# A two-layer hybrid decoder step: another order at three places between stages (modulation loads, first projection units, the pool of split weights)

## The chip, the cores and the metric

The kernel runs on one core of a Trainium2 chip, as one launch. The metric is device time in microseconds of that launch; lower is better. A core has five engines with queues of their own: TensorE (PE; the load of its stationary operand is listed apart as PEld), VectorE (DVE), ScalarE (ACT), GpSimd (POOL) and SyncE (SP), which here issues nearly all DMAs. Each engine runs its queue in order; semaphores order the queues against one another.

## The reference

Two layers are computed for 1024 prompt tokens and 32 sample tokens (8 sequences of 4), feature width 1024, in float32. Per layer, cut to what matters here:

```python
mod = (jax.nn.silu(c) @ lp["w_ada"] + lp["b_ada"])[:, None, :]
sh1, sc1, g1, sh2, sc2, g2 = jnp.split(mod, 6, axis=-1)
h = rmsnorm(x, lp["norm1_g"]) * (1.0 + sc1) + sh1
p = split_cols(h @ lp["w_in"])
...
x = x + g1 * (concat(o_a, o_b, o_c, o_d) @ lp["w_out"])
h2 = rmsnorm(x, lp["norm2_g"]) * (1.0 + sc2) + sh2
x = x + g2 * ((silu(causal_dwconv(h2 @ lp["ffn_w_gate"])) * (h2 @ lp["ffn_w_up"])) @ lp["ffn_w_down"])
```

The four head groups are an RG-LRU, differential attention, sparse attention (an indexer scores all keys, the 256 best are kept) and gated linear attention. The outputs are the last norm of x and the new caches and states.

## The kernel before

**Data.** x is kept transposed, xT[p, k, t], eight tiles of 128 features by 1056 tokens; the 1056 tokens go in three chunks, CHK = 384, 384 and 288 (the last holds 256 prompt tokens and the 32 sample tokens), or in nine tiles TOK of 128 (the last of 32). A float32 product is made of three: the weights and the activations are each split in a rounded part hi and a rest lo, and hi·hi, hi·lo and lo·hi are summed in PSUM.

**Weights.** `unit` (L426) loads a block of 1024 x 256 weights in two halves ("wr", two buffers, a DMA from SP each), ScalarE rounds each half to wh (L434), GpSimd subtracts to get wl (L435). wh and wl have two buffers each. `dense_t` (L456) and `dense_c` (L444, matmuls at L451) give output features by tokens, one chunk at a time, 24 matmuls; `dense_n` (L462, matmuls at L471) gives tokens by features, one token tile at a time, 24 matmuls.

**Head (L517 to L612).** The nine token tiles of x are loaded (512 KB each, "xn") and transposed to xT (L547); beside them go 20 small vector loads (`load_vectors`, L251) and the first four units of the modulation (`ada`, L317; 16 loads "adaw" of 512 KB in rows of 2 KB, 32 matmuls at L330, and a small transpose at L336, L338). Squares are summed per chunk (`add_square`, L346). Then `norm_chunk` (L385) runs for chunks 0, 1 and 2: the reciprocal root (`rstd_chunk`, L361), a VectorE product per feature tile (L392), and `split` (L375), which writes hi on ScalarE (L382, or L378 and L379) and lo on VectorE (L383) or GpSimd (L380), in turns. The six parts of h lie in a pool opened where the loads' pool was.

**Input projection (L633 to L1207).** Its pool "hp" is opened there, and holds wh and wl too. First comes `misc_unit` (L679): 128 odd columns (gla_a, idx_k, idx_w) for all three chunks, then nine transposes (L691), evacuations (L694, L695), rotations and stores, by token tile. Then `nat_unit("idx_q")` (L651): nine token tiles, each evacuated (L660), rotated (L499 to L503) and stored (L665). The tile "nat" that is stored has three buffers, shared by both units. The rotation table "c_rope" is loaded into hp. Then follow the units lru_x, lru_gate, dsa_q and so on. After each of their chunks or tiles, and after each idx_q tile, `background` (L639) advances other streams: the indexer, the top-k of the prompt and the samples, and in layer 0 one piece of the remaining modulation (16 matmuls, "late").

**Output projection and MLP (L1992 to L2198).** w_out is split into four units in two right-hand pools, wo and wo2; the MLP's pool "ffp" holds its own wh and wl. The last norm chunk of the MLP's input (L2115) is issued with the first gate unit (L2114). Eleven blocks q of 256 hidden features run gate, up and, one block late, down: 24 groups (8 feature tiles, 3 chunks) of 6 matmuls at L2082, each added to xT on VectorE (`add_residual`, L480). The last two blocks' down products are done together, 12 matmuls a group, chunk by chunk, with the squares (L354, L355) and the next layer's norm behind each chunk (L2193 to L2197):

```python
                if pend is not None and q < 10:
                    w = down_w(pend[0])
...
                    last = [(down_w(9), pend[1]), (down_w(10), mids)]
...
            for c in range(3):
                for m in range(8):
                    down_mc(m, c, last)
                    add_square(xT, m, c, acc, sqt)
                finish(c)
```

**What sets the order.** The program's order gives priorities, and the framework's planner, which runs a timeline simulation as it builds, makes each engine's fixed queue out of them. Pools lie on two stacks; a tile of a new pool waits for the tiles that lay at its place.

Of the kernel before, what the change touches and what calls it, by code (L numbers as in the profile page):

```python
# [71 lines left out]
def _const_tables():  # L72
    """Tables and 0/1 masks that depend on shapes alone, one float32 array of 128 rows."""
# [67 lines left out]
def trunk(ctx, tc, io, out, dbg=None, depth=DEPTH, stop=99):  # L141
# [19 lines left out]
    def banks(**bufs):  # L161
        """the eight banks of PSUM dealt out anew: single ones by name, pairs as s; d and e stay open while they can."""
# [10 lines left out]
    def advance(gens, n=1):  # L173
        """n steps of the first streams of the list that are not done; False when none is left."""
        for _ in range(n):
            while gens:
                try:
                    next(gens[0])
                    break
                except StopIteration:  # L180
                    gens.pop(0)
        return bool(gens)

    def pipeline(gens, depth):
        """the streams one after another, up to depth of them at once, a step of each per step, oldest first."""
# [20 lines left out]
    def evac(dst, src, ratio=(1, 1)):  # L206
        """PSUM to SBUF on ScalarE or VectorE in turns."""
# [41 lines left out]
    vecp = ctx.enter_context(tc.tile_pool(reuse_waits="tile", name="vec", bufs=1))  # L249

    def load_vectors(l, wp):  # L251
        v = {}
        if True:
# [39 lines left out]
            pa = bank("m")  # L293
# [5 lines left out]
            # half the convolution: silu(2 z) = z (1 + tanh(z))  # L299
            dve.tensor_scalar(V[:, 128:216], V[:, 128:216], 0.5, None, op0=mult)  # L300
            pc = bank("m")
# [15 lines left out]
    def ada(adap, l, u0, u1, nb=2, ne=1, nk=8):  # L317
        """units of 512 columns of the modulation, in pieces of nk * 128 rows and 1024 / nk columns."""
        w_ = 1024 // nk
        for u in range(u0, u1):  # L320
# [13 lines left out]
            pm = bank("m")  # L334
            for j in range(4):
                pe.matmul(pm[:, 9 * j:9 * j + 9], lhsT=ev[:, j * 128:j * 128 + 128], rhs=sum4,  # L336
                          start=True, stop=True)
            dve.tensor_tensor(mods[l][:, 4 * u:4 * u + 4, :], pm[:, :36].rearrange("p (j c) -> p j c", j=4),  # L338
                              vecs[l]["b_ada"][:, 4 * u:4 * u + 4, None].to_broadcast([128, 4, 9]), op=add)

# [5 lines left out]
    def add_square(x, k, c, acc, tmp):  # L346
        """acc += x^2 for the features of tile k, chunk c of the tokens."""
# [13 lines left out]
    def rstd_chunk(get, acc, c):  # L361
# [3 lines left out]
        # 1 / sqrt(v), v = sum / D + eps: ScalarE's value, then a Newton step  # L365
# [9 lines left out]
    def split(hi, lo, y, bias, k):  # L375
        """hi + lo = y + bias, lo on VectorE or GpSimd in turns."""
# [8 lines left out]
    def norm_chunk(get, x, acc, c, A, mod, base, hi, lo):  # L385
        """hi + lo = modulated norm of x, chunk c of the tokens."""
# [16 lines left out]
    def part(wp, c, z):  # L403
        """tile for part z of [features, tokens], chunk c of the tokens."""
# [7 lines left out]
    def raw_piece(rp, aps, width, i, n, nr):  # L412
        """rows of piece i of n of a [1024, width] block of weights; aps: list of (column, AP)."""
# [11 lines left out]

    def unit(wp, rp, aps, width, n=2, first=None):  # L426
        """hi and lo of a block of weights, [128, 8, width]."""
# [10 lines left out]
    def split2(parts_, c, g, raw):  # L438
        """the parts of two tiles of features, chunk c of the tokens."""
# [4 lines left out]
    def dense_c(w, j, h, c, order=range(8)):  # L444
        """out^T[m, t] = sum_k w[k, m] h[k, t] for 128 columns m and chunk c of the tokens."""
# [16 lines left out]
    def dense_n(w, i, h):  # L462
        """out[t, m] = sum_k h[k, t] w[k, m] for token tile i, 256 columns."""
# [12 lines left out]
    def add_residual(x, m, c, p, gate, mod):  # L476
        """x += gate * p for 128 features m and token chunk c."""
# [48 lines left out]
    with tc.tile_pool(reuse_waits="tile", name="xin", bufs=9) as xi:  # L526
# [13 lines left out]
        for i, (t0, n) in enumerate(TOK):  # L540
# [9 lines left out]
            if i % 2:  # L550
                next(ups[i // 2])
# [3 lines left out]
        while advance(vl):  # L555
            pass
# [1686 lines left out]
```

## Time and profile before

| | |
|---|---|
| time, median of 3 runs (lowest to highest) | 3930.11 us (3924.64 to 3934.86) |
| span of the profiled execution, first to last instruction | 3915.6 us |
| own time of the profiled execution | not listed apart from its span; the median is 14.5 us above the span |
| busy: PE, DVE, ACT, POOL | 3549.8, 2461.3, 1510.5, 1387.5 us |
| mean granted TensorE clock (1 is 2.4 GHz) | 0.952 |

The profile lists what each engine was busy with and what its idle time waited for. Busy shares are averages over stages with different limits, so the reading below goes stage by stage. Matmuls overlap, so the mean duration of one is longer than the step from one to the next.

### The profile page before, as it was taken

The numbers are of one execution on the slowest core, as the hardware profiler recorded it, in microseconds if no ns is written. First come the engines' busy times: TensorE is split into PE (matmuls) and PEld (weight loads), VectorE is DVE, ScalarE is ACT, GpSimd is POOL, SyncE is SP. The second block draws the span as 40 slices with busy tenths as digits, with TensorE's granted clock in tenths as the row PEclk, the third lists the DMA queues.
The fourth block names the chain that finished last, engine by engine and source line by source line (L and its number), as shares of the span: only waits on it lengthen the run. The fifth ranks groups of instructions, "written<-read, shape, count | busy, mean of one in ns | idle before, by whom it ended". The sixth has DMA issues, their size and how long they took to land.

```text
span 3915.6 us, 66494 instructions
## 1 busy us (share of the span) xinstructions
PE 3549.8 (91%) x26004; PEld 3202.2 (82%) x26004; DVE 2461.3 (63%) x5614; ACT 1510.5 (39%) x3058; POOL 1387.5 (35%) x1241
## 2 busy tenths in 40 slices
PE   5998867899898999999979988688997899999998
PEld 3887765577788999999979877556786899999997
DVE  6379989676445454445553999996753545555555
ACT  4345644376533211211243556535763322112122
POOL 2344226534233222222323642564333222323231
PEclk7999988999999999999989999899998999999999
DMA  6542334546431333321113222546546011111111
GB/s 223 158 129 87 112 116 144 181 131 187 165 103 44 98 103 94 96 76 44 55 65 89 87 87 79 155 150 195 150 155 207 28 44 44 49 39 54 44 44 56
DMA packets 351155, 407.77 MB, mean 104 GB/s; under 512 B 93455, under 2 KB 294909, under 8 KB 350682
## 3 DMA queue, kind: packets, MB, share of 16 engines
q1 hardware_dynamic: 311930, 265.09, 22.5%
q0 software_dynamic: 38912, 138.43, 11.1%
q8 instruction: 205, 3.36, 0.4%
q14 instruction: 108, 0.88, 0.1%
HBM read 354.32 MB, written 58.04 MB: 105 GB/s over the span
## 4 chain that ended last, share of the span: by engine, by line
PE 66%; DVE 19%; DMA 4%; ACT 4%; issue 4%; POOL 1%; SPq 1%; another core or an unknown queue 0%; DVEq 0%; ACTq 0%; POOLq 0%
PE d L451 32%; PE m L2082 13%; PE m L1601 3%; PE d L471 2%; DVE tkb L799 2%; PE d L1334 2%; DVE tku L799 2%; PE e L1340 2%; PE e L1363 2%; PE m L1596 1%; PE d L330 1%; PE g L1700 1%; PE m L719 1%; DVE nat L499 1%; DMA xn<-in_x_prompt_dram 1%
## 5 line engine op out<-in xcount | busy, mean ns | idle before, releaser
L451 PE MATMUL d<-h,wh 128*128 128x384 f32 (+1 forms) x5856 | 1413.2, 327 | 69.2 <-ACT wh L434 26.2
L451 PEld LDWEIGHTS d<-h,wh 128*128 128x128 f32 x5856 | 1038.8, 192 | 86.2 <-ACT wh L434 31.5
L451 PE MATMUL d<-h,wl 128*128 128x384 f32 (+1 forms) x2928 | 947.4, 327 | 3.6 <-POOL wl L435 3.6
L451 PEld LDWEIGHTS d<-h,wl 128*128 128x128 f32 x2928 | 559.5, 191 | 7.8 <-POOL wl L435 6.7
L435 POOL TENSOR_TENSOR wl<-wr,wh 128x1024 fp32r<-128x1024 f32 (+1 forms) x172 | 376.7, 2208 | 357.5 <-ACT wh L434 345.5
L471 PE MATMUL d<-wh,h 128*128 128x256 f32 (+1 forms) x2304 | 462.5, 297 | 34.0 <-ACT nat L664 18.1
L480 DVE SCALAR_TENSOR_TENSOR xT<-m,mod,xT 128x384 f32<-128x384 f32 (+1 forms) x480 | 273.1, 572 | 228.8 <-PE m L2082 228.3
L471 PEld LDWEIGHTS d<-wh,h 128*128 128x128 f32 (+1 forms) x2304 | 372.0, 192 | 54.6 <-ACT nat L664 22.7
L2082 PE MATMUL m<-mh,wdh 128*128 128x384 f32 (+1 forms) x1056 | 349.2, 331 | 0.4 <-DVE xT L480 0.4
L2163 POOL TENSOR_TENSOR ml<-z,mh 128x384 fp32r<-128x384 f32 x132 | 133.5, 1031 | 605.7 <-ACT mh L2162 605.7
L2082 PE MATMUL m<-ml,wdh 128*128 128x384 f32 (+1 forms) x1056 | 343.3, 325 | 0.0
L2082 PE MATMUL m<-mh,wdl 128*128 128x384 f32 (+1 forms) x1056 | 342.1, 325 | 0.0
L471 PE MATMUL d<-wl,h 128*128 128x256 f32 (+1 forms) x1152 | 339.8, 295 | 0.0
L434 ACT CAST wh<-wr 128x1024 fp32r<-128x1024 f32 (+1 forms) x172 | 157.9, 955 | 238.7 <-PE d L451 174.5
L2134 DVE COPY fs<-G 128x2 f32<-128x2 f32 x44 | 50.9, 1158 | 285.2 <-ACT G L2130 285.2
L471 PEld LDWEIGHTS d<-wl,h 128*128 128x128 f32 (+1 forms) x1152 | 221.7, 192 | 8.0 <-issue 5.7
L2130 ACT COPY G<-d 128x384 f32<-128x384 f32 x132 | 57.1, 443 | 418.1 <-PE d L451 387.5
L2082 PEld LDWEIGHTS m<-mh,wdh 128*128 128x128 f32 x1056 | 199.6, 189 | 9.3 <-issue 7.0
L2082 PEld LDWEIGHTS m<-ml,wdh 128*128 128x128 f32 x1056 | 199.2, 189 | 1.5 <-issue 1.2
L2082 PEld LDWEIGHTS m<-mh,wdl 128*128 128x128 f32 x1056 | 199.3, 189 | 0.0
L2072 POOL TENSOR_TENSOR wdl<-wr,wdh 128x1024 fp32r<-128x1024 f32 x44 | 105.0, 2418 | 263.8 <-ACT wdh L2071 263.8
L1334 PE MATMUL d<-c_ident,kv 128*128 128x128 f32 x1024 | 171.8, 291 | 10.6 <-ACT s_wT L210 4.0
(532 smaller groups left out, 6740.4 us busy)
## 6 DMA issues: line engine op xcount, KB each, us to landing
adaw<-in_w_ada_dram SPq DMA_DIRECT2D x96, 512.0 KB
wr<-in_w_in_dram SPq DMA_DIRECT2D x48, 512.0 KB
wr<-in_ffn_w_gate_dram SPq DMA_DIRECT2D x44, 512.0 KB
wr<-in_ffn_w_up_dram SPq DMA_DIRECT2D x44, 512.0 KB
wr<-in_ffn_w_down_dram SPq DMA_DIRECT2D x44, 512.0 KB
xd<-xT SPq DMA_DIRECT2D x16, 528.0 KB
wr<-in_w_out_dram SPq DMA_DIRECT2D x32, 256.0 KB
mix<-mx SPq DMA_DIRECT2D x24, 256.0 KB
```

The source lines that it names most:

```text
L434: act.copy(hi[:, ks, :width], raw[:, :, :width])
L435: pool.tensor_tensor(lo[:, ks, :width], raw[:, :, :width], hi[:, ks, :width].bitcast(F32), op=sub)
L451: pe.matmul(pd, lhsT=w[a][:, k, j * 128:j * 128 + 128], rhs=h[b][c][:, k, :], start=(q == 0), stop=(q == 23))
L471: pe.matmul(pd[:n, :256], lhsT=h[b][c][:, k, t0:t0 + n], rhs=w[a][:, k, :], start=(q == 0), stop=(q == 23))
L480: dve.scalar_tensor_tensor(x[:, m, t0:t0 + n], p[:, :n], mod[:, gate + m, 0:1], x[:, m, t0:t0 + n], op0=mult, op1=add)
L799: dve.tensor_scalar(scratch[:, :n], src[:, s], thr[:, j:j + 1], None, op0=OP.is_ge, op1=add, accum_out=cnt[:, j:j + 1])
L1334: pe.transpose(pm[:, z_ * 128:z_ * 128 + 128], kg[:, j, f * 128:f * 128 + 128], ident)
L1340: pe.matmul(pd[32 * j:32 * j + 32, c], lhsT=Q[:, f, b_].rearrange("p c t -> p (c t)"), rhs=kt[:, j, f, :], start=(f == 0), stop=(f == 1))
L1601: pe.matmul(po[:, 64 * z:64 * z + 64], lhsT=wT[:, x * 128:x * 128 + 128], rhs=vn[:, kb, :], start=(kb == 0), stop=(kb == i))
L2072: pool.tensor_tensor(lo[:, z_, :], raw, hi[:, z_, :].bitcast(F32), op=sub)
L2082: pe.matmul(pd, lhsT=a, rhs=b, start=(n == 0), stop=(n == len(ops) - 1))
L2163: pool.tensor_tensor(ml[:, cs], z[:, cs], mh[:, cs].bitcast(F32), op=sub)
```

## The change

It does six things, all in the order of work and the place of tiles; every matmul stays.

- The first modulation is loaded by `ada_first`: eight loads of 1 MB, in rows of 8 KB, and its 32 matmuls run by row block over four PSUM banks. The loads, and the small vector loads, are issued after the third of the nine x tiles, ahead of the other six.
- `misc_unit` and the idx_q unit become `first_units`: chunk by chunk, the odd columns, three idx_q tiles, then the three transposes with their rotations and stores. It calls no `background`.
- wh and wl move from hp and ffp to a pool of their own, opened beside wr (`weights`), which spans output projection, MLP and the next input projection. The first two w_out units use it; wo2 is gone.
- The unit of odd columns is split before its stage (`mw`), not only loaded.
- In layer 0 the down product of block 9 is done like the others, and only that of block 10 runs chunk by chunk with the norm.
- The vectors' transposes take a "d" bank in the head.

```diff
@@ ada / ada_first
-            pm = bank("m")
...
+            ada_rows(l, u, ev)
+    def ada_first(adap):
+        pa = [bank("m") for _ in range(4)]
+        for k in range(8):
+            w = adap.tile([128, 2048], F32, name="adaw", bufs=8)
+            sp.dma_start(w, io["w_ada"][0][k * 128:(k + 1) * 128, 0:2048])
+            q = k % 4
+            for u in range(4):
+                pe.matmul(pa[u][32 * q:32 * q + 32, :], lhsT=cT[:, k, :], rhs=w[:, 512 * u:512 * u + 512],
+                          start=(k < 4), stop=(k >= 4))
+            yield
+        for u in range(4):
+            ev = adap.tile([128, 512], F32, name="adae", bufs=4)
+            evac(ev, pa[u])
+            ada_rows(0, u, ev)
@@ head
-        ups = [ada(xi, 0, u, u + 1, 16, 4, 2) for u in range(4)]
+        ups = [ada_first(xi)]
...
-            advance(vl, 3)
-            if i % 2:
-                next(ups[i // 2])
...
+            if i == 2:
+                advance(ups, 4)
+                advance(vl, 20)
+                advance(ups, 4)
+                while advance(vl):
+                    pass
+                while advance(ups):
+                    pass
...
-    mraw = raws(wrp, misc_aps(0), 128)
+    wrpool, wrp, wpool, wp_ = weights("0")
+    mw = unit(wp_, wrp, misc_aps(0), 128)
@@ input projection
-            w = unit(hp, wrp, [(0, col(name))], 256)
+            w = unit(wp_, wrp, [(0, col(name))], 256)
...
+        def first_units():
             rope_t.append(const("rope", where=hp).rearrange("p (i w) -> p i w", i=9))
+            w = unit(wp_, wrp, [(0, col("idx_q"))], 256)
             mtp = tc.tile_pool(reuse_waits="tile", name="mt", bufs=1)
             mt = mtp.__enter__().tile([128, T], F32, name="mt")
+            for c, (c0, cn) in enumerate(CHK):
+                act.copy(mt[:, c0:c0 + cn], dense_c(mw, 0, h, c))
+                for i in range(3 * c, 3 * c + 3):
+                    nat_tile("idx_q", w, i)
+                for i in range(3 * c, 3 * c + 3):
+                    t0, n = TOK[i]
+                    pm = bank("m")
+                    pe.transpose(pm[:n, :128], mt[:, t0:t0 + n], ident)
...
             sp.dma_start(stt["gla_a"], mt[0:16, :])
...
-        misc_unit()
-        nat_unit("idx_q")
+        first_units()
@@ output projection and MLP
-        wrpool = tc.tile_pool(reuse_waits="tile", name=f"wr{l + 1}", bufs=2)
-        wrp = wrpool.__enter__()
+        wrpool, wrp, wpool, wp_ = weights(f"{l + 1}")
...
-                    ws_.append(unit((wo, wo2)[u // 2], wo, [(0, io["w_out"][l][:, u * 256:u * 256 + 256])], 256, 4))
+                    ws_.append(unit((wp_, wo)[u // 2], wo, [(0, io["w_out"][l][:, u * 256:u * 256 + 256])], 256, 4))
...
-            w0 = unit(fp_, wrp, [(0, io["ffn_w_gate"][l][:, 0:256])], 256, first=graw)
+            w0 = unit(wp_, wrp, [(0, io["ffn_w_gate"][l][:, 0:256])], 256, first=graw)
...
-                if pend is not None and q < 10:
+                if pend is not None and (q < 10 or l + 1 < depth):
...
-                    last = [(down_w(9), pend[1]), (down_w(10), mids)]
+                    last = ([] if l + 1 < depth else [(down_w(9), pend[1])]) + [(down_w(10), mids)]
...
-                mraw = raws(wrp, misc_aps(l + 1), 128)
+                mw = unit(wp_, wrp, misc_aps(l + 1), 128)
```

## Rows read from the trace of the kernel before

**Rows 1.** The page: shares of the chain that ended last, by engine.

```profile
PE 66%; DVE 19%; DMA 4%; ACT 4%; issue 4%; POOL 1%; SPq 1%; another core or an unknown queue 0%; DVEq 0%; ACTq 0%; POOLq 0%
```

**Rows 2.** Windows: stretch, length, busy of PE, PEld, DVE, ACT, POOL; clock, DMA.

```profile
20.00:40.00 20.00, 14.67 (x87) 7.18 (x87) 11.35 (x24) 9.34 (x19) 1.05 (x2) 1.00 1.01 368
...
48.00:100.00 52.00, 23.73 (x64) 14.84 (x63) 42.42 (x78) 27.34 (x64) 23.96 (x30) 0.62 0.52 161
...
150.00:260.00 110.00, 110.00 (x997) 100.68 (x996) 62.61 (x82) 53.49 (x97) 35.13 (x35) 1.00 0.56 164
260.00:560.00 300.00, 256.78 (x1760) 231.17 (x1758) 288.17 (x780) 156.83 (x317) 115.24 (x114) 0.94 0.28 87
...
1994.00:2025.00 31.00, 27.73 (x179) 26.90 (x177) 27.47 (x61) 17.75 (x35) 6.66 (x6) 1.00 0.19 75
2025.00:2045.00 20.00, 1.52 (x3) 0.73 (x4) 14.30 (x35) 9.81 (x22) 5.69 (x7) 0.54 0.26 103
2045.00:2066.00 21.00, 20.78 (x125) 20.09 (x125) 3.16 (x5) 6.30 (x15) 12.80 (x12) 0.87 0.52 146
2066.00:2074.00 8.00, 1.67 (x5) 0.61 (x5) 2.19 (x13) 1.88 (x12) 2.72 (x14) 0.82 0.47 119
```

**Rows 3.** Timeline of the head: start, length, what, idle before and its releaser.

```profile
45.78 0.68 PE L547 MATMUL d<-c_ident,xn 32*128 32x32 f32 x8
...
47.84 0.19 DVE L338 TENSOR_TENSOR mod<-m,V 128x36 f32<-128x36 f32 x1
...
56.28 0.61 ACT L382 ACTIVATE h<-ny,mod 128x384 fp32r<-128x384 f32 x1
...
98.57 0.40 ACT L400 CAST h<-ny 128x256 fp32r<-128x256 f32 x1 [0.23 <-DVE ny L399]
```

**Rows 4.** Chain: first lru_x chunk, layer 0; idx_q tiles, lru_x, layer 1.

```profile
149.77 4.17 PE d L451 x24
...
2087.89 8.72 PE d L471 x72
2096.61 4.16 PE d L451 x24
```

**Rows 5.** Groups by shape: 1990 to 2045, 2044 to 2100, 100 to 150.

```profile
L480 DVE SCALAR_TENSOR_TENSOR xT<-m,mod,xT 128x384 f32<-128x384 f32 x8 | 4.9, 614 | 1.1 <-PE m L2082 1.0
...
L499 DVE TENSOR_TENSOR nat<-rraw,c_rope 128x256 f32<-128x256 f32 x8 | 4.8, 601 | 7.1 <-ACT rraw L660 6.3 <-DMA st_iw<-nat 0.7
...
L330 PE MATMUL d<-adaw,cT 128*32 128x128 f32 x144 | 5.8, 278 | 1.3 <-DVE nat L499 1.0 <-DMA adaw<-in_w_ada_dram 0.3
```

**Rows 6.** Line L872, last step of the top-k, both layers.

```profile
L872 DVE TENSOR_SCALAR mk<-tkb x5: 317/2446/2540, 527.1 to 556.4; 128x384 bf16<-128x384 bf16 x1, 128x512 bf16<-128x512 bf16 x1, 128x640 bf16<-128x640 bf16 x1, 128x768 bf16<-128x768 bf16 x1
...
L872 DVE TENSOR_SCALAR mk<-tkb x3: 363/386/415, 2484.8 to 2500.0; 128x768 bf16<-128x768 bf16 x1, 128x896 bf16<-128x896 bf16 x1, 128x1024 bf16<-128x1024 bf16 x1
```

**Rows 7.** Timeline of the boundary between the layers.

```profile
1970.94 0.42 PE L2082 MATMUL m<-mh,wdh 128*128 128x384 f32 x1
...
2024.24 0.30 PE L2082 MATMUL m<-mh,wdl 128*128 128x288 f32 x1
...
2043.80 0.40 ACT L400 CAST h<-ny 128x256 fp32r<-128x256 f32 x1 [0.25 <-DVE ny L399]
...
2045.07 0.33 SPq L220 DMA_DIRECT2D c_rope<-in_const_dram  x1
```

**Rows 8.** Waits on PE, 1970 to 2100: total, times, longest.

```profile
PE m L691 <- ACT nat L695: 5.8, 4, 4.4
```

**Rows 9.** Timeline of the start of the MLP, layer 0, then layer 1.

```profile
1195.07 2.53 POOL L435 TENSOR_TENSOR wl<-wr,wh 128x1024 fp32r<-128x1024 f32 x1 [2.69 <-DVE ny L370]
...
1195.41 2.52 DVE L372 TENSOR_TENSOR rb<-rb,ny 128x288 f32<-128x288 f32 x1
...
1210.74 1.25 PE L451 MATMUL d<-h,wh 128*128 128x288 f32 x3 [8.01 <-ACT h L400]
...
3124.72 1.25 PE L451 MATMUL d<-h,wh 128*128 128x288 f32 x3 [7.42 <-ACT h L400]
```

More of the change, by code (lines that the diff above doesn't have):

```diff
@@ L333, in ada, with ada_rows @@
                 yield
-            pm = bank("m")
[L335 to L339, printed above, removed]
+            ada_rows(l, u, ev)
+    def ada_rows(l, u, ev):
+        pm = bank("m")
+        for j in range(4):
+            pe.matmul(pm[:, 9 * j:9 * j + 9], lhsT=ev[:, j * 128:j * 128 + 128], rhs=sum4,
+                      start=True, stop=True)
+        dve.tensor_tensor(mods[l][:, 4 * u:4 * u + 4, :], pm[:, :36].rearrange("p (j c) -> p j c", j=4),
+                          vecs[l]["b_ada"][:, 4 * u:4 * u + 4, None].to_broadcast([128, 4, 9]), op=add)
+    def ada_first(adap):
[12 more added lines that the diff above has]
+            ada_rows(0, u, ev)
     def scales(g, mod, base, A):
@@ L424, in raws, with weights @@
         return [raw_piece(rp, aps, width, i, 2, 2) for i in range(2)]
+    def weights(name):
+        rp = tc.tile_pool(reuse_waits="tile", name="wr" + name, bufs=2)
+        wp = tc.tile_pool(reuse_waits="tile", name="w" + name, bufs=2)
+        return rp, rp.__enter__(), wp, wp.__enter__()
     def unit(wp, rp, aps, width, n=2, first=None):
@@ L554, in trunk @@
                     add_square(xT, k, i // 3, acc, sqt)
-        while advance(vl):
-            pass
-        for g in ups:
-            next(g, None)
+            if i == 2:
[6 more added lines that the diff above has]
+                    pass
     identb = cp.tile([128, 128], BF, name="identb")
@@ new lines, in first_units @@
+            for c, (c0, cn) in enumerate(CHK):
[3 more added lines that the diff above has]
+                for i in range(3 * c, 3 * c + 3):
+                    t0, n = TOK[i]
+                    pm = bank("m")
+                    pe.transpose(pm[:n, :128], mt[:, t0:t0 + n], ident)
+                    nat = hp.tile([128, CWM], F32, name="nat", bufs=3)[:, :256]
+                    raw = hp.tile([128, 256], F32, name="rraw", bufs=2)
+                    act.copy(raw[:n, 0:32], pm[:n, 32:64])
+                    act.copy(nat[:n, 32:40], pm[:n, 64:72])
+                    tmp = hp.tile([128, 256], F32, name="rtm", bufs=2)
+                    rope(nat[:n, 0:32], raw[:n, 0:32], i, n, 32, tmp[:n, 0:32], rope_t[0])
+                    sp.dma_start(st["idx_k"][t0:t0 + n, :], nat[:n, 0:32])
+                    sp.dma_start(st["idx_w"][t0:t0 + n, :], nat[:n, 32:40])
@@ L2003, in trunk @@
         ff = hpl.__enter__()
-        wrpool = tc.tile_pool(reuse_waits="tile", name=f"wr{l + 1}", bufs=2)
-        wrp = wrpool.__enter__()
+        wrpool, wrp, wpool, wp_ = weights(f"{l + 1}")
         with ExitStack() as es:
-            nm_, wo2, wo = (es.enter_context(tc.tile_pool(reuse_waits="tile", name=k, bufs=2, side="right"))
-                            for k in ("nm", "wo2", "wo"))
+            nm_, wo = (es.enter_context(tc.tile_pool(reuse_waits="tile", name=k, bufs=2, side="right"))
+                       for k in ("nm", "wo"))
             def staged(c, n):
```

69 lines of the change are left out of this document (28 added, 41 removed).

## The prediction

> **What bounds it now.** I read the chain first, then windows by stage, then timelines where TensorE stops. The chain is TensorE's for 66% [rows 1], and where it is busy throughout, at full clock, this change takes no matmul away; so I look for places where it waits. In the windows [rows 2] there are two large ones. In the head, 48 to 100 us, PE is busy 23.73 of 52 us at a clock of 0.62 while VectorE is busy 42.42: the three norm chunks feed it too slowly. Between the layers, 2025 to 2045, PE works 1.52 of 20 us at 0.54 while VectorE finishes the last norm; from 2066 to 2074 it works 1.67 of 8. Two small ones lie at the start of each MLP, 8.01 and 7.42 us [rows 9]. Saved time must then pass the stage behind. From 150 us PE is busy 110.00 of 110 us and then VectorE 288.17 of 300 [rows 2]; both depend on the first projection units alone, so the whole of it moves earlier. I count from the first lru_x chunk: 149.77 in layer 0, 2096.61 in layer 1 [rows 4].
>
> **The head, start.** Moving the modulation ahead of six x tiles leaves the bytes as they are, some 12.7 MB (8.4 of weights, 4.3 of x). The DMA ran at 368 GB/s and a share of 1.01 there with rows of 2 KB [rows 2], so I give rows of 8 KB no gain. The Trainium skill ("DMA: Bandwidth & Descriptors", Bandwidth) says to batch transfers to 1 MiB for three quarters of peak and lists 425 GB/s for the largest; by that the 12.7 MB would take 4.6 us less and the sum would be 3866. The 512 KB transfers here already ran at 368.
> What changes is what is last. Now the modulation is ready at 47.84, after the last x tile's transpose at 45.78, and the first part of h is written at 56.28 [rows 3]: in between lie the scale, the root, and a queue of squares. Afterwards modulation, root and squares of chunk 0 are done while x still lands. But chunk 0's hi part lies where I reckon the last x tiles lie, in the order in which the tiles are taken, so it cannot be written before about 46.5. That is 10 us earlier; the ends are 0 and, if it lies elsewhere, some 14.
> VectorE then has the same three norms plus the rotations of six idx_q tiles, which now come before the end of the last norm: 12 operations at 0.6 us [rows 5], 7 us. So the last part of h comes 3 us earlier than 98.57 [rows 3], near 96. SP carries the 20 vector loads ahead of x4 to x9; each is small and runs beside the 1 MB loads, so nothing is charged.
>
> **The head, behind the norm.** Now 50.8 us pass from the last part of h to lru_x (149.77 less 98.97). Afterwards one odd chunk and three idx_q tiles are left: 24 matmuls at 4.17/24 us times 288/384, 3.1 us, and 72 in 8.72 us [rows 4], 11.8 together at full clock and 23.7 at half. The clock has been 0.62 in this stage [rows 2] and more work fills it, so I take the middle, 18: 33 us less. The rest of the first units must fit under the norms: two odd chunks and six tiles, 26 us at full clock, in the 50 from 46 to 96; they fit at half clock too, barely.
> Nine pieces of later modulation leave this stretch (144 matmuls, 5.8 us busy [rows 5]) and follow later. From lru_x to the last step of the top-k, layer 0 takes 556.4 less 149.8, 406.6 us, with 23 such pieces; layer 1 takes 2500.0 less 2096.6, 403.4, with none [rows 4, 6]. So 23 cost at most 3.2 us and nine 1 us; the cover is the VectorE stretch, and without it they would cost 6.
> Head: -3 - 33 + 1 = -35 us; ends -49 and -17 (no earlier start, 7 for the rotations, half clock, 3 for the pieces).
>
> **Between the layers.** TensorE's sum is unchanged; block 9's pass just comes first. It takes 96 matmuls of 384 columns and 48 of 288, 23 us at the same step, so the chunk-wise pass begins not at 1970.94 [rows 7] but near 1994. VectorE's work behind it is 27.47 + 14.30 us [rows 2] and 9.6 for the 16 operations of chunk 0 that it now does before 1994 (at 0.6, L480's 614 ns [rows 5]): 51.4. Done densely it ends at 2045.4; with the 5.7 us of idle that 2025 to 2045 shows, at 2051, 7 later than 2044.2 [rows 7]. The extra 24 additions of block 9 hide under its matmuls.
> What TensorE does meanwhile is the gain. Odd chunks 0 and 1 fit before. The idx_q weights, though, need the wh buffer that block 10 gives up with its last matmul, near 2036 at VectorE's pace, and the rotation table seems to lie over the norm's scratch: its load is issued at 2045.07 [rows 7], right behind the norm, and will be again, some 4 us to landing (0.65 MB at 368 GB/s is 1.8; I take double for issue and completion). Four tiles can run without it, two in the evacuation buffers and two in PSUM. Left after the table: 3.1 + 5 x 2.9 = 18 us. lru_x then starts at 2051 + 4 + 18 = 2073 instead of 2097: -24.
> Against it: the splits of odd columns and idx_q, which now run where VectorE idles (3.16 of 21 us busy [rows 2]), move under its chain. A GpSimd split of 2.53 us stretched a VectorE operation to 2.52 [rows 9], where its like takes some 0.5. Two whole and two half splits: at most 7.6 us, and I take all of it, the chain being dense. Boundary: -16 us; ends -24 and +11 (the chain 23 later, nothing run ahead, locks on top).
>
> **The start of the MLP.** The first gate block's buffer is now free when the first w_out unit ends, several feature tiles before the end of that pass, so its split and the first up split can go earlier. They now sit in the last norm chunk: 2.52 us for L372 is one such collision [rows 9], 2 us too long, and I take the other half of that split to cost as much. Taking both away brings the norm's end 4 us forward in each layer: -8; ends 0 and -15 (both waits gone, 8.01 + 7.42). If the norm is not faster, TensorE only waits longer there, since it starts gate earlier.
>
> **Sum.** -35 - 16 - 8 = -59. The profiled span of 3915.6 becomes 3857; with the 14.5 us between span and median, 3930.1 becomes 3871.
>
> **Rivals.**
> *The boundary gives nothing* (0.20). VectorE's chain moves by the whole 23 us and nothing of idx_q runs ahead. For it: VectorE, 27.47 of 31 us, sets the pace there [rows 2]; against: some of its idle is waiting for TensorE. +3 to +11 for -16: about 3894. The Trainium skill ("SBUF — State Buffer", Who interferes with whom) says that a VectorE operation with two SBUF inputs and a GpSimd one that reads SBUF take a pair of ports by turns, whole instructions long; [rows 9] bear that out, 2.53 beside 2.52.
> *The head keeps its norm* (0.12). The part of h still waits for x, the clock stays half: -17 for -35, 3889. That rows of 8 KB do nothing belongs here, and is my assumption already. With the rival above, 3912.
> *The store buffers take turns with TensorE* (0.07; the other side). idx_q tiles and odd tiles now alternate over the three nat buffers, 18 a layer, six turns, and the transposes stand between the tiles in TensorE's queue. Now the wait shows for the odd tiles alone, 4.4 us at the longest [rows 8], and 6.3 us of idle from 2066 to 2074 [rows 2]. If every turn cost that, 12 x 6.3 = 76 us would come on: 3947, slower. It decides from 5.9 us a turn ((59 + 12)/12). Against it: 6.3 us of matmuls lie between two turns.
> The rest (0.06) is the planner dealing another stage out differently; the two layers' 406.6 and 403.4 us say that it deals alike.
>
> **Numbers.** The forecast has 0.55, and by itself 3850 to 3892. From the ends, -88 (3842) and -6; the range goes from 3842 to 3918, over the first two rivals, and leaves the third out. 0.3%, 12 us, is about what a measurement here can tell from no change. Faster by more: the forecast and most of two rivals, 0.84; within it 0.08, both rivals together or a mild third; slower 0.08.
>
> **What would show it.** Right: modulation ready before the last x transpose and the first h near 46; the first lru_x chunk near 114; between the layers the last norm 7 us later and lru_x 16 us earlier behind the start of block 9's pass than now; idx_q matmuls before the last norm ends; no split inside the MLP's last norm chunk. Wrong: first h still past 55; PE waits on nat at every transpose; the last norm between the layers more than 15 us later with TensorE idle beside it; VectorE no longer dense behind lru_x, so that what was gained is lost there.

## The result, and the profile after

| | before | after |
|---|---|---|
| median (lowest to highest), us | 3932.49 (3924.64 to 3936.61) | 3954.66 (3950.60 to 3964.66) |
| profiled execution: own time / span, us | - / 3915.6 | 3950.6 / 3948.8 |
| mean granted TensorE clock | 0.952 | 0.946 |

The ratio is 1.0062, interval 1.0043 to 1.0081: the change makes the kernel slower, where I forecast 3871 us and a range of 3842 to 3918. The two profiled spans differ by 33.2 us, the medians by 22.2: a part of the differences below belongs to the two executions that were profiled. (After's own time lies 1.8 us above its span, and in the later comparisons the kernel before has medians of 3916.6 to 3918.8. So the 14.5 us that I put between its span and its median were no fixed part of the time: executions of the same kernel differ by that much.)

To find where the time went I cut the span at four points in each layer, each read from one tile of the trace: the first store of lru_x, the last write to the top-k's tile tkb, the last load of w_out, the last mh (the rounded hidden features) of the MLP. "Mixers" are the four head groups. The columns after "after" are experiments that come below.

| us from the point before | before | after | head | units | pool | after_kb9 | after_kb9_vec | units_rows_kb9 |
|---|---|---|---|---|---|---|---|---|
| start to lru_x, layer 0 | 156.9 | 133.5 | 160.8 | 124.2 | 153.6 | 134.5 | 122.6 | 123.3 |
| to the end of the top-k | 407.8 | 431.5 | 408.1 | 429.2 | 405.7 | 431.7 | 431.5 | 432.5 |
| to w_out (the mixers) | 558.6 | 546.5 | 567.4 | 549.0 | 558.7 | 545.0 | 553.8 | 543.8 |
| to the last mh (output, MLP) | 849.7 | 854.9 | 853.4 | 853.5 | 854.8 | 852.9 | 856.3 | 854.1 |
| to lru_x, layer 1 (boundary) | 131.2 | 134.8 | 131.5 | 126.8 | 137.7 | 135.0 | 134.9 | 125.5 |
| to the end of the top-k | 395.0 | 400.1 | 394.9 | 395.4 | 394.8 | 395.1 | 400.0 | 396.8 |
| to w_out (the mixers) | 536.8 | 566.6 | 544.0 | 553.3 | 535.8 | 543.5 | 540.2 | 543.2 |
| to the last mh | 802.9 | 806.0 | 805.9 | 805.1 | 805.6 | 806.1 | 807.9 | 804.8 |
| to the end | 76.7 | 74.9 | 75.3 | 77.8 | 75.1 | 75.1 | 75.0 | 75.1 |
| span | 3915.6 | 3948.8 | 3941.3 | 3914.3 | 3921.8 | 3918.9 | 3922.2 | 3899.1 |

After less before: -23.4, +23.7, -12.1, +5.2, +3.6, +5.1, +29.8, +3.1, -1.8; sum +33.2. lru_x does start 23 us earlier, and all of it is gone by the end of layer 0's top-k. The boundary gives nothing. The largest term, +29.8, lies in the mixers of layer 1, where the source was not touched. Each column is one execution, so a few us prove little: before, pool and before_kb9 run the same order up to lru_x, and it comes at 156.9, 153.6 and 153.9.

**Head.** SyncE's queue, timeline of after (start, length, what):

```profile
3.67 2.17 SPq L350 DMA_DIRECT2D adaw<-in_w_ada_dram  x4
...
8.73 0.27 SPq L291 DMA_DIRECT2D va_rows<-in_lru_conv_w_dram  x1
11.21 0.23 SPq L291 DMA_DIRECT2D va_rows<-in_lru_conv_b_dram  x1
...
18.75 0.23 SPq L291 DMA_DIRECT2D va_rows<-in_lru_lambda_dram  x1
...
23.26 2.10 SPq L350 DMA_DIRECT2D adaw<-in_w_ada_dram  x4
...
25.88 5.07 SPq L568 DMA_DIRECT2D xn<-in_x_prompt_dram  x5
```

What SP waited for in it (total, times, longest):

```profile
SPq L291 <- DMA adaw<-in_w_ada_dram: 9.0, 4, 2.3
```

The same stretch, 0 to 48 us, in the DMA view (40 slices of 1.2 us, busy tenths and GB/s), and the first and the last step of the head's norm on ScalarE:

```profile
DMA  0247999999999980001489999999999999921404
GB/s 0 57 66 263 379 416 451 430 423 410 437 423 416 437 315 5 8 5 38 125 142 389 410 430 423 437 423 430 438 370 404 406 413 406 304 20 32 82 6 52
```

```profile
L402 ACT ACTIVATE h<-ny,mod x12: 492/602/615, 62.6 to 104.5; 128x384 fp32r<-128x384 f32 x8, 128x256 fp32r<-128x256 f32 x4
...
L420 ACT CAST h<-ny x1: 404/404/404, 109.3 to 109.3; 128x256 fp32r<-128x256 f32 x1
```

Behind four loads of 1 MB a small load comes off SP only every 2.5 us, because SP waits for landings. By the trace's semaphores the program lets each DMA of SP wait until the one eight places before it has landed, and the issues at 11.21, 13.69, 16.19 and 18.75 follow the landings of the four 1 MB loads by 0.02 us. Twelve more small loads then take until 23.26, when the fifth 1 MB load is issued. From 18.0 to 22.8 us, slices 16 to 19, the DMA engines move 5 to 38 GB/s, in the next two 125 and 142. The first part of h is written at 62.6, where it was at 56.28, and the norm ends at 109.3, where it ended at 98.57 [rows 3].

**Stages.** Windows of after (columns as in [rows 2]):

```profile
20.00:40.00 20.00, 15.70 (x42) 4.14 (x41) 1.36 (x3) 0.58 (x1) 0.00 (x0) 0.83 0.83 325
48.00:100.00 52.00, 36.36 (x174) 29.35 (x173) 44.28 (x74) 31.03 (x65) 20.96 (x21) 0.68 0.52 166
...
2040.00:2056.00 16.00, 0.00 (x0) 0.00 (x0) 10.91 (x22) 7.32 (x17) 5.59 (x7) 0.50 0.12 42
```

TensorE does work beside the head's norm now, 36.36 of 52 us for 23.73 [rows 2]. VectorE, which worked 11.35 us from 20 to 40, now works 1.36. And between the layers TensorE stands still for 16 us on end.

From lru_x to the top-k's first step, in before and then in after, same columns:

```profile
156.90:275.40 118.50, 117.43 (x1077) 107.49 (x1076) 70.90 (x94) 57.33 (x100) 37.11 (x39) 1.00 0.56 164
```

```profile
133.50:271.10 137.60, 130.72 (x1185) 116.78 (x1184) 71.33 (x101) 61.93 (x113) 42.52 (x46) 0.98 0.55 159
```

The first of six query blocks' scores on VectorE, in before and then in after (shortest, median, longest; first and last start):

```profile
L761 DVE TENSOR_SCALAR sc<-irl,wix x6: 402/620/917, 156.0 to 255.5; 128x384 f32<-128x384 f32 x1, 128x512 f32<-128x512 f32 x1, 128x640 f32<-128x640 f32 x1, 128x768 f32<-128x768 f32 x1
```

```profile
L793 DVE TENSOR_SCALAR sc<-irl,wix x6: 487/587/782, 153.7 to 250.2; 128x384 f32<-128x384 f32 x1, 128x512 f32<-128x512 f32 x1, 128x640 f32<-128x640 f32 x1, 128x768 f32<-128x768 f32 x1
```

VectorE has the same 71 us of work there, but the stretch is 19.1 us longer: TensorE works 13.3 us more in it, on 108 more matmuls that stand ahead of the top-k's start. (50 of them are of the later modulation, 38 of the projections, 20 of the scores themselves.) The first score comes only 2.3 us earlier than in before, 20.2 us behind lru_x, where it was level with it. The top-k itself then takes 4.6 us more.

**Boundary.** Timeline of after, GpSimd, VectorE, ScalarE and TensorE in turn:

```profile
2027.33 5.00 POOL L461 TENSOR_TENSOR wl<-wr,wh 128x1024 fp32r<-128x1024 f32 x2 [0.83 <-ACT wh L460]
...
2055.11 0.72 POOL L421 TENSOR_TENSOR h<-ny,h 128x256 fp32r<-128x256 f32 x1
...
2027.82 4.92 DVE L412 SCALAR_TENSOR_TENSOR ny<-xT,A,rb 128x384 f32<-128x384 f32 x2
...
2055.87 0.38 ACT L691 ACTIVATE rraw<-d 128x256 f32<-128x256 f32 x1 [0.86 <-POOL h L421]
2056.15 0.47 ACT L716 COPY mt<-d 128x384 f32<-128x384 f32 x1
...
2056.30 0.58 PE L497 MATMUL d<-wh,h 128*128 128x256 f32 x1 [17.72 <-ACT rraw L691]
```

One odd chunk and one idx_q tile were computed ahead (24 matmuls each, the last near 2034). They fill the two PSUM banks "d", and neither bank is emptied (rraw, mt) before the norm's very last operation, L421 at 2055.11, has read the norm's scratch. TensorE waits 17.72 us.

**Layer 1's mixers.** Last gathers of the samples and last transposes of the prompt, in before and then in after, there with the w_out loads, and the chain right behind:

```profile
L245 POOL DMA_INDIRECT kv<-in_cache_dsa_v_dram,idx x32: 935/939/1388, 2743.5 to 2974.2; - x32
...
L1263 PE MATMUL m<-c_ident,oa_dsa x16: 272/273/282, 2962.7 to 2973.8; 128*128 128x128 f32 x16
```

```profile
L245 POOL DMA_INDIRECT kv<-in_cache_dsa_v_dram,idx x32: 933/937/2825, 2769.0 to 3010.6; - x32
...
L1295 PE MATMUL m<-c_ident,oa_dsa x16: 272/273/328, 2972.7 to 2983.4; 128*128 128x128 f32 x16
...
L439 SPq DMA_DIRECT2D wr<-in_w_out_dram x16: 367/378/462, 3017.0 to 3067.9; - x16
```

```profile
3026.90 3.24 DMA mix<-s_oT
```

The prompt is done at 2983.4; the samples' last gather is issued 27.2 us later, and the chain runs through their store (mix<-s_oT). I call these 27.2 us the samples' tail. In before both ended together: 2974.2 for the gather, 2973.8 for the prompt. (The first expectations give 24 and 51 us for it; they count from an earlier step of the prompt, its last masked scores at 2950.3 and 2959.8.) Over all seventeen kernels of this document, the three with a tail of 27 us or more in layer 1 take 562.0 to 573.7 us in its mixers, and the others, with 7.4 at most, 535.8 to 553.6.

### The profile page after: what moved, and what is told of

The parts are those of the page before. It is cut to its first block, busy times and chain, and to the rows that moved or that the text cites. A ratio compares the mean times of both kernels' runs of the same rounds, so it can differ in the third digit from the quotient of the medians.

```text
span 3948.8 us, 66548 instructions
## 1 busy us (share of the span) xinstructions
PE 3566.9 (90%) x26004; PEld 3214.4 (81%) x26004; DVE 2478.8 (63%) x5654; ACT 1514.1 (38%) x3058; POOL 1395.5 (35%) x1241
## 5 line engine op out<-in xcount | busy, mean ns | idle before, releaser
L506 DVE SCALAR_TENSOR_TENSOR xT<-m,mod,xT 128x384 f32<-128x384 f32 (+1 forms) x504 | 286.7, 572 | 225.5 <-PE m L2113 225.0
L2194 POOL TENSOR_TENSOR ml<-z,mh 128x384 fp32r<-128x384 f32 x132 | 133.3, 1028 | 605.5 <-ACT mh L2193 605.5
```

The source lines that it names most:

```text
L506: dve.scalar_tensor_tensor(x[:, m, t0:t0 + n], p[:, :n], mod[:, gate + m, 0:1], x[:, m, t0:t0 + n], op0=mult, op1=add)
L2194: pool.tensor_tensor(ml[:, cs], z[:, cs], mh[:, cs].bitcast(F32), op=sub)
```

## The experiments

Ratios are against the kernel before, run beside each on the same chip.

**The parts alone.** Each is the kernel before with one part of the change's diff.

*head*: `ada_first` and its place in the loop over x.

```diff
-        ups = [ada(xi, 0, u, u + 1, 16, 4, 2) for u in range(4)]
+        ups = [ada_first(xi)]
```

> The kernel before with the head's part alone (modulation in 1 MB loads ahead of x3 to x8; units and pools as before). Theory A, 'the index keys set layer 0': the index scores start after the last chunk of the odd columns; here these stay ahead of idx_q, so idx_k is read back as many us earlier than 120.3 as lru_x is earlier than 156.9, and the top-k ends that much earlier than 564.7: if the last norm comes 3 to 6 us earlier, the total falls by 3 to 6 us. Theory B, 'the head itself is worse': TensorE's queue holds the modulation's matmuls ahead of the transposes of x3 to x8, the last norm comes no earlier than 98.6, and the total is 0 to +10 us. Theory C, 'the samples are dealt differently': the gap between the last prompt step and the last kv gather of layer 1 (24 us in before, 51 in after) moves by over 10 us though nothing in layer 1 was edited.

Ratio 1.0096 (1.0071 to 1.0120). The norm ends at 102.5, lru_x comes 3.9 us later, and everything up to the top-k's end is shifted by 4.2: theory B for the head, but not for the total, which rose by 32 us. The rest of the +25.7 us in span is in the mixers (+8.8 and +7.2) and the output and MLP stages (+3.7, +3.0), with nothing edited there. The samples' last gather, 0.4 us behind the prompt in both layers of before, is now 19.4 and 7.4 behind: a part of theory C.

*units*: `first_units` in place of the odd columns' unit and the idx_q unit, with its weights in hp.

```diff
-        misc_unit()
-        nat_unit("idx_q")
+        first_units()
```

> The kernel before with the first two projection units chunk by chunk alone (head and pools as before). Theory A, 'the index keys set layer 0': idx_k is read back later than 120.3 (its last chunk now stands behind nine idx_q tiles), lru_x starts 10 to 20 us earlier than 156.9, and the top-k still ends within 4 us of 564.7. Layer 0 gains nothing, the total is within -5 to +10 us unless layer 1's samples move. Theory of the prediction: the top-k ends 15 to 25 us earlier and the total falls by as much. Theory C, 'the samples are dealt differently': layer 1's last kv gather falls 20 us or more behind the prompt's last step against before, and the total is +15 to +35 us.

Ratio 0.9996 (0.9983 to 1.0009). lru_x starts 32.7 us earlier in layer 0 (in the full change only 23.4), but the way to the top-k's end is 21.4 us longer: it ends 11.3 us earlier, between theory A and that of the prediction. In layer 1 that way is unchanged (395.4). The boundary is 4.4 us shorter, and by the end of layer 1's top-k the kernel is 21.1 us ahead. The mixers take 16.5 of that back, without a tail (0.4 us, as in before), so theory C is not the reason; what is, is not shown.

*pool*: the shared pool, `mw`, and block 9's down product ahead.

```diff
-                if pend is not None and q < 10:
+                if pend is not None and (q < 10 or l + 1 < depth):
```

> The kernel before with the shared pool of split weights alone (block 9's down pass ahead in layer 0, odd columns' weights split in the MLP; head and units as before). My prediction gave the start of the MLPs -8 and the norm between the layers +7: total -5 to +5 us. If the norm between the layers ends over 15 us later than 2044.2 and nothing runs beside it, +10 us. Theory C: layer 1's samples end 20 us or more later than before against the prompt, total +20 to +40.

Ratio 1.0012 (1.0001 to 1.0024). The boundary costs 6.5 us more, and output and MLP cost 5.1 and 2.7 more. The last norm between the layers ends 87.9 us behind the last mh, where it took 70.8. The samples' tail stays at 0.4: not theory C.

**The index keys.** *kfirst*: the changed kernel, with the odd columns' tiles of a chunk ahead of its idx_q tiles.

```diff
                 for i in range(3 * c, 3 * c + 3):
-                    nat_tile("idx_q", w, i)
-                for i in range(3 * c, 3 * c + 3):
                     t0, n = TOK[i]
...
+                for i in range(3 * c, 3 * c + 3):
+                    nat_tile("idx_q", w, i)
```

> The changed kernel, with the index keys' transposes of a chunk ahead of that chunk's idx_q tiles instead of behind them. Theory A: idx_k of layer 0 is read back near 125 instead of 139.6 and that of layer 1 near 2092 instead of 2105.8; the index scores start near 135 to 145 instead of 153.7, the top-k of layer 0 ends 8 to 18 us earlier than 565.0, and the total falls by about as much, 8 to 25 us below the changed kernel. Rival, 'paced by the program's order': the scores are advanced two steps per chunk of lru_x, so they start no earlier and the top-k ends within 3 us of 565.

Ratio 1.0033 (1.0022 to 1.0045). The keys are read back at 124.6 instead of 139.6 and the first score comes 8.9 us earlier, but the last score (269.7 for 269.9) and the end of layer 0's top-k (565.0) stay as in the change: the rival is right, theory A falls for layer 0. Layer 1's top-k comes 11.3 us earlier, half of it already at lru_x. That this kernel beats the change by 24 us of span lies for 13.0 in layer 1's mixers (553.6 for 566.6).

*units_k_kb9*: the same order in units, with samples at 0.9 steps (below).

> The run units_kb9 with the index keys of a chunk ahead of its idx_q tiles (as in kfirst). In kfirst the top-k of layer 0 did not move (565.0) and that of layer 1 came 11 us earlier, 6 of them already at lru_x. Theory A, weakened: idx_k is read back 10 to 15 us earlier in both layers; layer 0's top-k ends within 3 us of 557.5, layer 1's 3 to 8 us earlier than 2478.2; total -8 to +2 us against units_kb9 (3907.8).

Ratio 0.9992 (0.9982 to 1.0001), against 0.9976 for units_kb9. Layer 0's top-k ends at 559.0 (557.5). In layer 1 the way from lru_x is 3.6 us shorter, but lru_x comes later, and the end is 4.0 later (2482.2): no gain.

**The nine pieces of later modulation.** *units_bg*: background is called again after each idx_q tile.

```diff
                     nat_tile("idx_q", w, i)
+                    background()
```

> The kernel of the run units, with the call of background after each idx_q tile put back (in layer 0 nine pieces of the later modulation run there again, as before; in layer 1 nothing is left to run at that point). In units layer 0 went from the first lru_x store to the last top-k step in 429.2 us against 407.8 in before, layer 1 in 395.4 against 395.0. Theory D, 'the nine pieces': lru_x comes a few us later than in units (124.2), the stretch falls back to 408 to 412, the top-k ends 5 to 15 us earlier than 553.4, the total is 5 to 15 us less unless the mixers are dealt worse. Rival E, 'TensorE's stretch ahead of VectorE's': the scores are paced by the calls and VectorE is full from 260 us whatever stands before it; the top-k still ends between 550 and 557 and the stretch stays over 420.

Ratio 1.0045 (1.0022 to 1.0068). lru_x is 9.7 us later, the way to the top-k's end 7.1 shorter (422.1), so that end is 2.6 later: rival E. The pieces alone are not what eats the gain: what the way gains by their going back, lru_x loses. Layer 1's mixers take 573.7 us, with the samples 30.9 us behind the prompt.

**The pace of the scores.** *units_tk3_kb9*: three score steps a call in place of two, beside units_kb9.

```diff
-TK = 2
+TK = 3
```

> The run units_kb9 with the index scores advanced three steps instead of two per call of background. Theory G, 'the scores are paced': in layer 0 of units and of the changed kernel TensorE is busy 130 us between lru_x and the top-k's first step (117 in before), with more of the projection ahead of the scores; at three steps the top-k's first step comes 15 to 30 us earlier than 263.5 and its last 8 to 25 us earlier than 557.5, in layer 1 the last step 5 to 20 us earlier than 2478.2, and the total falls by 8 to 30 us. Rival, 'VectorE's sum': from the first score to the last step VectorE has the same work and no idle to give back; the last step moves by under 5 us in both layers.

Ratio 0.9998 (0.9988 to 1.0007), where units_kb9 has 0.9976: the total did not fall, it rose by some 8 us. Windows of this run, lru_x to the top-k's first step, the top-k, and what is left behind it:

```profile
124.30:236.80 112.50, 106.79 (x854) 92.33 (x853) 59.37 (x77) 57.88 (x99) 31.63 (x29) 0.94 0.48 140
236.80:542.90 306.10, 252.32 (x1876) 224.41 (x1876) 291.20 (x818) 156.32 (x323) 113.18 (x114) 0.91 0.33 103
543.00:568.00 25.00, 23.73 (x148) 23.49 (x146) 12.90 (x74) 11.55 (x29) 1.24 (x3) 0.99 0.20 62
```

Theory G holds for layer 0's top-k: with 854 matmuls instead of 1191 ahead of it (units and units_kb9), the top-k starts 26.7 us earlier and ends 14.6 earlier than in units_kb9. But TensorE's projections, which ended before the top-k, now end 25 us behind it, near 568. Layer 0's projection stage is held by two engines nearly equally: relieving VectorE handed the end to TensorE. Layer 1's top-k, at 397.4 us behind lru_x (400.2), moves by 2.8 us only.

**The samples' pace.** *after_kb9*, *units_kb9* and *before_kb9* change one number in the changed kernel, in units and in before; *units_kb10* sets it to 1.0.

```diff
-KB = 0.8
+KB = 0.9
```

> The changed kernel with the samples advanced 0.9 steps per prompt step instead of 0.8. Theory C, 'the samples are late': in layer 1 of the changed kernel the last kv gather starts at 3010.6, 27 us behind the last prompt step (2983.4); with 12% more sample steps per prompt step it falls to within 5 us of that, w_out's first load comes 15 to 27 us earlier against the top-k's end, and the total is 10 to 25 us less. Rival, 'the samples are late because the selection is late': the selection's last step (2642.6) holds them, and the total moves by less than 5 us.

Ratio 1.0016 (1.0004 to 1.0028) where the change has 1.0062. After_kb9's rows:

```profile
L245 POOL DMA_INDIRECT kv<-in_cache_dsa_v_dram,idx x32: 932/937/1128, 2749.3 to 2980.4; - x32
...
L1295 PE MATMUL m<-c_ident,oa_dsa x16: 272/273/280, 2960.7 to 2973.0; 128*128 128x128 f32 x16
```

The tail shrinks from 27.2 to 7.4 us, layer 1's mixers from 566.6 to 543.5, and the span by 29.9 (the median, by the ratios, by some 18). So most of the slowdown goes with this tail, though the new pace also reorders the rest of the stage.

> The run units with the samples at 0.9 steps per prompt step. There layer 1's top-k ends 21 us earlier than in before but w_out is loaded only 3 us earlier. If the samples lose it: w_out 5 to 15 us earlier in layer 1, total 5 to 15 us below units (3915.5). If the GLA stage loses it (its last step 15 us earlier than before where its first is 30 us earlier): total within 4 us of units.

Ratio 0.9976 (0.9965 to 0.9987). The median is 7.7 us below that of units, within what I gave the samples' pace. But in layer 0 the mixers take 4.1 us less and in layer 1 only 2.0, w_out does not come 5 us earlier there, and units had no tail that could shrink: the total fits that theory, the place does not, and the cause stays open.

> The kernel before with 0.9 sample steps per prompt step. In before the samples end with the prompt in layer 1 (2974.2 against 2973.8 us): a faster pace has nothing to give there, and the total is within 5 us of before. If 0.9 is simply better for every deal, it falls by 8 us or more, and then the gain of units_kb9 over before is not the units'.

Ratio 1.0000 (0.9987 to 1.0014): in before there is no tail, and the pace gives nothing.

> The run units with 1.0 sample steps per prompt step (0.8 in units, 0.9 in units_kb9). The samples' last gather comes 10 us or more ahead of the prompt's last step in both layers, so nothing is left to gain from the pace; if the pace is what matters, the total is within 4 us of units_kb9 (3907.8), if the order of dealing matters beside it, it differs by more either way with no tail of samples to blame.

Ratio 0.9961 (0.9948 to 0.9974), median 3903.38: about 4 us under units_kb9 (6 by the ratios), no more than these intervals can part. The samples did not end as early as I expected: 13.3 us ahead of the prompt in layer 0, but 1.7 behind it in layer 1.

**The head inside the change.** *nohead*: the changed kernel with the old head.

```diff
-        ups = [ada_first(xi)]
+        ups = [ada(xi, 0, u, u + 1, 16, 4, 2) for u in range(4)]
```

> The changed kernel with the head as before (modulation in 512 KB pieces behind x). The planner deals the mixers of both layers in the same order as in the changed kernel, so only the head's own price shows. By the runs head (lru_x 3.9 us later than before) and units (lru_x at 124.2 against 133.5 in the changed kernel): lru_x at 122 to 127, the top-k of layer 0 ends 4 to 10 us earlier than 565.0, the total is 4 to 10 us less than the changed kernel's. If the head is a gain, as I forecast, lru_x is later than 140 and the total more.

Ratio 1.0081 (1.0055 to 1.0107), which does not tell it from the change: inconclusive as a time. In the trace the head costs what the expectation said: lru_x at 126.7, layer 0's top-k at 558.4, 6.6 us earlier, span 10.6 less. GpSimd's queue in layer 1's mixers has nearly the same order as in the change, and the samples the same tail, 27.4 us.

*after_kb9_vec*: after_kb9 with the vector loads behind the modulation.

```diff
             if i == 2:
-                advance(ups, 4)
-                advance(vl, 20)
-                advance(ups, 4)
...
+                advance(ups, 8)
+            if i >= 2:
+                advance(vl, 4)
```

> The run after_kb9 with the eight 1 MB loads of the modulation issued in a row, and the 20 vector loads four at a time behind x3 to x8, instead of between the fourth and the fifth 1 MB load. Theory F, 'SyncE's queue opens a hole': in the changed kernel the vector loads hold SP from 5.96 to 23.26 us, and the DMA queue stands nearly still from about 18 to 25 us; without that the modulation's last matmul ends 6 to 9 us earlier than 40.7, the last norm of layer 0's head ends 5 to 9 us earlier than 109.3 (102.5 in the run head, 98.6 in before), lru_x starts as much earlier than 134.5; the total falls by 2 to 7 us, since the VectorE stretch behind takes some back. Rival, 'TensorE's order': the transposes of x3 to x8 still stand behind the modulation's 32 matmuls, so the norm's end moves by under 3 us.

The DMA view, 0 to 48 us, and the norm's last step:

```profile
DMA  0347999999999999999999992857889793030589
GB/s 0 58 76 263 396 403 451 430 437 423 430 416 430 416 430 423 423 430 416 416 410 430 394 394 79 218 229 161 319 245 330 219 343 19 15 80 15 78 314 258
```

```profile
L420 ACT CAST h<-ny x1: 404/404/404, 99.5 to 99.5; 128x256 fp32r<-128x256 f32 x1
```

Theory F: the hole is gone, the norm ends 10.7 us earlier than in after_kb9 (110.2), and lru_x and layer 0's top-k both come 12 us earlier: what the norm gains passes whole. Yet the ratio is 1.0028 (1.0016 to 1.0040): the mixers of layer 0 take 8.8 us more and the MLP 3.4, and at the last mh nothing is left.

**What passes through.** *units_rows_kb9*: units_kb9 with that mended head; *units_rows_k_kb9* has the keys first as well.

> The run units_kb9 with the modulation in 1 MB loads ahead of x3 to x8 and the vector loads behind them (the head that after_kb9_vec mended). Layer 1's mixers are dealt in the same order as in units_kb9, layer 0's are not. If that head is a gain by itself: the last norm of the head ends 5 to 10 us earlier than 100.3, lru_x starts as much earlier than 124.5, the top-k of layer 0 ends 4 to 10 us earlier than 557.5. Theory C, 'the deal': the stretch from the top-k's end to the last w_out load of layer 0 (544.9 us in units_kb9; 541.5 to 569.5 over all runs) decides whether it is kept; total 3890 to 3915. If gains ahead of the mixers do reach the end, 3898 to 3904.

Ratio 0.9964 (0.9951 to 0.9978), median 3902.00, the lowest of all: it beats both kernels. But the mended head is no gain: the norm ends at 100.3 as in units_kb9, lru_x 1.2 us earlier. Of the 11.7 us of span that it has over units_kb9, 8.1 lie in layer 1's mixers (543.2 for 551.3), with the same order in GpSimd's queue: the order alone does not fix that stage's time. Its profiled execution was its fastest, and that of units_kb9 nearly the slowest of ten; the medians differ by 5.8 us.

> The same with the index keys ahead of the idx_q tiles of a chunk. It deals layer 1 otherwise than units_rows_kb9. Theory C: its projections end within 4 us of units_rows_kb9's in both layers (measured at the top-k's end against the start of the stage), and what the totals differ by, up to 15 us either way, lies between the top-k's end and the last w_out load.

Ratio 0.9977 (0.9968 to 0.9987). Layer 0's top-k ends 1.2 us later than in units_rows_kb9, its mixers take 554.5 for 543.8: there the difference lies where theory C puts it. In layer 1 the top-k ends at 2486.6 for 2476.0, which the stages before have brought along (from lru_x it takes 395.5 us for 396.8).

## Why the prediction was wrong

- **Head, start (-3):** wrong, +10.7. The step that failed is "each is small and runs beside the 1 MB loads, so nothing is charged": the small loads hold SP, and the 1 MB loads behind them (after_kb9_vec shows it by moving them). The first h came at 62.6 and not near 46, past the 55 that I had named as a sign; that is 6.3 us of the 10.7. The other 4.4 lie between the first and the last h, where I had put 7 for the rotations. A second step failed with it: "modulation, root and squares of chunk 0 are done while x still lands". In the mended head the first h still comes at 53.9 to 55.5 and the norm ends at 98.6 to 100.3; in after_kb9_vec the small vectors are ready at 45.12 and the modulation right behind them, at 45.2 to 45.5, as the last x tile's copy ends. That rows of 8 KB give nothing was also my assumption; the rate is in fact somewhat higher, 410 to 437 GB/s in the full slices that hold 1 MB loads alone, while the full slices of before have 340 to 427 (the 368 of [rows 2] is a mean over 20 us). The Trainium skill ("DMA: Bandwidth & Descriptors", Bandwidth) lists 425 for its largest transfer, 16 MB issued from GpSimd, and the trace comes near it with 1 MB loads from SP. The 4.6 us that I worked out from it show nowhere: behind the loads the norm keeps VectorE busy for 44.28 of 52 us.
- **Behind the norm (-33):** right. From the norm's end to lru_x it is 24.2 us for 58.3, 34.1 less. (The working has a slip: 26 us at full clock are 52 at half and do not fit in 50.)
- **"The whole of it moves earlier":** wrong, +23.7 us of 431.5, and alone as large as the gain. A shift of the norm does pass whole (head, after_kb9_vec). What the first units gain does not: from the norm's end to the top-k's end it is 455.7 us for 466.1, so 10.4 of the 34.1 us arrive. From lru_x to the last score it takes 116.5 to 116.7 us in the four kernels with the old units and 133.3 to 138.4 in the twelve with the new ones at two score steps a call; at three it takes 110.8. The scores' share of TensorE is dealt per projection chunk, and more work stands ahead of them. kfirst rules out the keys as the sole cause and units_bg the nine pieces; why the first score falls 20 us behind lru_x is not shown.
- **The nine pieces (+1):** mis-sized by a misreading. The row of layer 0 in [rows 6] ends at 556.4 because it holds five of six steps; the sixth starts at 566.6. The stretch was 416.8 us and not 406.6, against 403.4 in layer 1, so the 23 pieces may cost up to 13.4 us there, not 3.2, and nine some 5. units_bg, with the nine back, is 7.1 us shorter.
- **Boundary (-16):** wrong, +3.6. My terms for the norm, +7 and 7.6 of locks, make 14.6, and it measured 17.4 behind the last mh (88.2 for 70.8): nearly right. What follows the norm was to fall by 31 us (24 and 7) and fell by 13.8, from 60.4 to 46.6. The lock is there: 5.00 us of GpSimd beside 4.92 for two VectorE operations that took 1.13 together elsewhere (at 2009.26). The Trainium skill ("SBUF — State Buffer", Who interferes with whom) states such a lock for a VectorE operation with two SBUF inputs beside a GpSimd one that reads SBUF, and the trace agrees. What failed is "two in the evacuation buffers and two in PSUM": the evacuation buffers wait for the norm's scratch, and one idx_q tile ran ahead, not four. That those buffers lie over the scratch is read from the wait alone; another place for them was not tried. The rival "the boundary gives nothing" (+3 to +11) has the size of it, but not quite the way: one tile did run ahead, and the chain moved by 17.4 us and not by 23.
- **Start of the MLP (-8):** wrong, +5.2 and +3.1 with the output stage. In layer 0 the splits have left the last norm chunk, and from its root (1189.8) to its end (1203.8) it takes 14.0 us for 16.8; but the way from chunk 0's root to that end grew to 74.1 from 71.1, and TensorE waits 9.6 us there for 8.01 [rows 9]. The collisions moved ahead instead of vanishing, GpSimd's split and two VectorE products in after:

```profile
1160.80 5.39 POOL L461 TENSOR_TENSOR wl<-wr,wh 128x1024 fp32r<-128x1024 f32 x2 [14.01 <-ACT wh L460]
...
1161.29 5.32 DVE L412 SCALAR_TENSOR_TENSOR ny<-xT,A,rb 128x384 f32<-128x384 f32 x2
```

- **"The planner deals alike" (0.06):** the largest miss, -12.1 and +29.8. I had compared two layers of one kernel, which says nothing of an edited one; nor did they agree, 416.8 and 403.4 us when read rightly. Over the runs (without units_tk3_kb9, where the projections run into them) the mixers take 541.5 to 567.4 us in layer 0 and 535.8 to 573.7 in layer 1. Three kernels whose GpSimd queue has nearly the same order in layer 1's mixers (the change, nohead, units_bg) have tails of 27.2, 27.4 and 30.9 us, and a faster pace of the samples cuts it to 7.4 in the change. Why the planner makes that order is not shown, nor what spreads the stage over 18 us in the kernels without such a tail.
- **The store buffers' turns (0.07):** did not happen. In the boundary TensorE waits for no nat store; the slower side was reached by another way.

## What to carry to other kernels

A stage counts as moved only when the engine that sets its end is fed earlier. Ask what deals that engine its work, and check it at the stage's last step. Where a planner orders everything anew after each edit, cut the trace at fixed points and account for the whole span before crediting an edit, and keep a margin for stages that nobody touched (here 26 to 38 us). Where each issue waits for an earlier landing, small loads issued between large ones cost the large ones their turn.

## What was not expected of the hardware

Loads of 1 MB in rows of 8 KB, issued from SP, ran at 410 to 437 GB/s in full slices. What looked like the chip holding SP for some 2.5 us a load is the program's own wait for the DMA eight places before: a 1 MB load landed about every 2.5 us here, and SP went on 0.02 us behind each.
